# RWKV pairs of a hybrid trunk: two column copies on ScalarE, bonus products emitted later, the inverse's stores on GpSimd's queue

## The chip, the cores and the metric

The kernel runs on one core of one Trainium2 chip. The metric is the device time of one execution in microseconds; lower is better. All data are float32, and the large products are made of three products of float32r halves each.

## What is computed

A trunk of two layers over 1024 tokens of width 1024. Each layer has a token mixer, a cross-attention into 256 memory tokens and a squared-ReLU MLP, each between two RMS norms. The change lies in layer 0's mixer, which runs RWKV-7 beside Mamba-2 behind one input projection. RWKV's part, cut to what matters:

```python
kk = hd(k * k_k);  kk = kk / max(norm(kk), 1e-12)
k  = k * (1.0 + (a - 1.0) * k_a)
def step(S, inp):                      # per head, 64 x 64 state
    r_t, w_t, k_t, v_t, a_t, b_t = inp # a_t = -kk, b_t = kk * a
    sa = einsum('bhvk,bhk->bhv', S, a_t)
    S = S * w_t + sa[..., None] * b_t + v_t[..., None] * k_t
    return S, einsum('bhvk,bhk->bhv', S, r_t)
...
y = y + sum(r_h * k_h * r_k, axis=-1, keepdims=True) * v_h   # the bonus
```

The recurrence is computed in 16 chunks of 64 tokens, with a 64x64 triangular inverse T for each chunk and head. The eight heads are worked on as four pairs of 128 channels.

## The kernel before

`mixer0` first runs 27 projections (`fm`): TensorE (PE) multiplies a weight tile with the normalised input, 48 products of 128x512 for each (`pd<-xth,wb`, `pd<-xtl,wb`; "dense products" below, 1280 in all). While these run, generators do the rest in small pieces. `rw_pair(p)` is the generator of pair p. It makes the decay factors, normalises k (two "norm products" with the block-of-ones matrix `ct`, evicted in L521, then Ln and Exp on ScalarE and a Newton step on VectorE, L490 to L493), forms the chunk operands `va` and `bk` (L534 to L553), multiplies r, k and r_k (L551, L554), and makes the **bonus products** (`rkw` times `xn`, L563), which L564 evicts with the factor v. Then four groups follow, each with eight AB products (`va`, `bk`; L575, evicted in L578) and 32 transposes, all of which `rw_chunk` reads later from DRAM scratch.

In `va[:, :, 1]`, each position of a chunk takes minus kk times the decay up to the position before; the first column of a chunk has no position before it, so it is minus kk alone (L546). `PC` keeps the decay of the whole chunk (L547). Both touch 16 columns, one for each chunk.

`rw_inverse(q)` waits for pairs 2q and 2q+1, loads the triangles (`As`), runs 31 steps of forward substitution on VectorE (L616, L617) and stores T: `Ts` and its transpose `As` (L620), twelve stores in all (L627). `rw_chunk(c)` then loads T of its chunk (L655, L656), and its first product is `cT` with `cAB`. After the projections come layer 1's K and V products of the cross-attention (`memside`; `ph<-mh,wb`), among which the chunks and the Mamba windows (`mb_window`) are interleaved, and then the output projection (`outproj`).

Two things set the order. A generator's `yield` gives a delay on a virtual clock `self.pt`, multiplied by `self.lag` (1.8 here), or a condition; `tick` runs the pieces that are due between two dense products. Then the tile framework's scheduler orders the instructions once more, by priorities that follow the order of emission. Each engine executes its own list strictly in order. DMAs are issued in order as well, by the engine that owns the queue: `nc.sync` (SP), `nc.scalar` (ScalarE, ACT) or `nc.gpsimd` (POOL). A waiting instruction holds whatever stands behind it on its engine.

Of the kernel before, what the change touches and what calls it, by code (L numbers as in the profile page):

```python
# [13 lines left out]
AF = mybir.ActivationFunctionType  # L14
# [7 lines left out]
CH = 64  # L22
# [33 lines left out]
class Trunk:  # L56
# [438 lines left out]
    def rw_pair(self, p, km, rm, va, lora, wa, rm64, pool, pt, S):  # L495


        nc, pc = self.nc, self.pc
        mul, add = ALU.mult, ALU.add
# [13 lines left out]
        v3 = lambda x: x.rearrange("p (c t) -> p c t", t=CH)  # L513
# [18 lines left out]
        va = va[0]  # L532
        eP = va[:, :, 3]
# [4 lines left out]
        kn = nt("xo")  # L538
# [4 lines left out]
        nc.scalar.copy(bk[CH:, :, 2], bk[CH:, :, 0])  # L543
        yield 3.5
        nc.vector.scalar_tensor_tensor(va[:, :, 1, 1:], v3(kn[:])[:, :, 1:], -1.0, eP[:, :, 0:CH - 1], mul, mul)
        nc.gpsimd.tensor_scalar(va[:, :, 1, 0], v3(kn[:])[:, :, 0], -1.0, None, mul)  # L546
        nc.gpsimd.tensor_copy(self.PC[:, p, :], eP[:, :, CH - 1])  # L547
        nc.gpsimd.tensor_tensor(eP, v3(rm[:]), eP, mul)
        k2 = nt("xn")
        nc.scalar.activation(k2[:], a[:], AF.Identity, scale=col(Q_KA), bias=self.oka[:, p:p + 1])  # L550
# [5 lines left out]
        self.st1(S["AR0"][:, :, p].rearrange("c p t -> p c t"), va[:, :, 1])  # L556
        self.st1(S["AR1"][:, :, p].rearrange("c p t -> p c t"), va[:, :, 3])
        yield lambda: 0.0 if self.v_done[0] > p else None
        yield 2.0
        bv = nt("xn")  # L560
        for sl in H:
            ps = self.psm()
# [28 lines left out]
    def rw_inverse(self, q, pool, pt, S):  # L591


        nc = self.nc
        yield lambda: 0.0 if self.rw_done[0] >= 2 * q + 2 else None
        B = 32
        block = lambda s: self.ed.tile([P, B, B], F32, name=self.n(s), tag="xo") if q else pool.tile([P, B, B], F32, name=self.n(s), tag=s)
        As = block("As")
        for a in range(2):
            for j in range(2):  # L600
                src = S["ABK"][:, CH * j:CH * j + CH, 2 * q + a, j, :]
                r0 = 64 * a + 32 * j
                for b in range(2):
                    v = src[:, B * b:B * b + B, B * b:B * b + B]
                    self.ld1(As[r0 + 16 * b:r0 + 16 * b + 16], v)
        Ts = block("Ts")
        yield 9.0
        nc.gpsimd.memset(Ts[:], 0.0)
        nc.gpsimd.memset(Ts[:].rearrange("p i k -> p (i k)")[:, 0:B * B:B + 1], 1.0)
        for k in range(B - 1):  # L610

            if k % 8 == 0:
                pr = pt.tile([P, B, B], F32, name=self.n("pr"), tag="tmp")
            n, m = B - 1 - k, k + 1
            pv = pr[:].rearrange("p i k -> p (i k)")[:, 0:n * m].rearrange("p (i j) -> p i j", j=m)
            nc.vector.tensor_tensor(pv, As[:, k, m:].unsqueeze(2).broadcast_to([P, n, m]), Ts[:, k, :m].unsqueeze(1).broadcast_to([P, n, m]), ALU.mult)  # L616
            nc.vector.tensor_tensor(Ts[:, m:, :m], Ts[:, m:, :m], pv, ALU.add)  # L617
            if k % 2:
                yield 0.4 + 0.004 * n * m
        nc.vector.tensor_copy(As[:], Ts[:].rearrange("p i k -> p k i"))  # L620
        for n_, x in enumerate((Ts, As)):
            for a in range(2):
                for j in range(2):
                    r0 = 64 * a + 32 * j
                    for b in range(n_ + 1):
                        dst = S["T"][n_, :, CH * j + B * b:CH * j + B * b + B, 2 * q + a, B * b:B * b + B]
                        (nc.scalar if b else nc.sync).dma_start(dst, x[r0 + 16 * b:r0 + 16 * b + 16])  # L627
        self.inv_done[0] += 1
        self.inv_t = self.pt + 5.0

# [1222 lines left out]
```

## Time and profile before

| | us |
|---|---|
| median of 3 runs (3078.88 to 3088.8) | 3080.72 |
| the profiled execution, in all | 3086.54 |
| its span, first to last instruction | 3084.8 |
| PE busy | 2924.9 (95%) |
| VectorE (DVE) busy | 1758.5 (57%) |
| ScalarE (ACT) busy | 1318.0 (43%) |
| GpSimd (POOL) busy | 656.5 (21%) |

The table of busy time tells which engine fills the span. A table by stretches tells where PE is not full, and which of its two clock levels was granted: 1.00 stands for 2.4 GHz, 0.50 for 1.2 GHz. The lists of waits and the timelines then name, for each gap of PE, what ended it.

### The profile page before, as it was taken

What the parts mean: (1) busy time and instruction counts of PE and PEld (TensorE: products, weight loads), DVE (VectorE), ACT (ScalarE), POOL (GpSimd) and SP (SyncE); (2) the same over time, 40 slices, a digit from 0 to 9 for tenths busy, and PEclk for the clock granted to TensorE, in tenths of its full rate; (3) what the DMA queues carried; (4) which work ended last, traced back from release to release, by engine and by line L of the source; (5) the groups of instructions that cost most, each with busy time, mean ns of one, the idle gap of its engine ahead of it and who ended that gap; (6) DMA issues with size and microseconds to landing.
All of it is one profiled execution on the core that took longest, in us unless ns stands there. A gap on an engine that the chain in (4) does not pass through costs nothing. (4 is left out here: it accounts for less than half of the span.)

```text
span 3084.8 us, 40050 instructions
## 1 busy us (share of the span) xinstructions
PE 2924.9 (95%) x15652; PEld 2381.1 (77%) x15652; DVE 1758.5 (57%) x2283; ACT 1318.0 (43%) x2096; POOL 656.5 (21%) x648
## 2 busy tenths in 40 slices
PE   8999999889989989999999999899999899999998
PEld 7776677777767867887887778777788678888876
DVE  7255776666643476664757723145653666657476
ACT  6455543445333345444443423133353444454433
POOL 1111131122212124443001200011221334440002
PEclk9999999999999989999999999999999899999999
DMA  7834476678552124447745533446331234468456
GB/s 257 276 88 127 123 197 196 209 255 266 184 186 69 69 89 147 152 151 267 239 138 163 195 106 103 123 132 219 116 129 62 82 120 151 150 217 283 138 164 224
DMA packets 274237, 506.00 MB, mean 164 GB/s; under 512 B 57328, under 2 KB 159664, under 8 KB 274048
## 3 DMA queue, kind: packets, MB, share of 16 engines
q1 hardware_dynamic: 218048, 309.89, 31.8%
q0 software_dynamic: 28448, 108.08, 9.2%
q10 hardware_dynamic: 27552, 85.47, 8.5%
q8 instruction: 123, 2.02, 0.3%
q14 instruction: 66, 0.54, 0.1%
HBM read 348.45 MB, written 154.89 MB: 163 GB/s over the span
## 5 line engine op out<-in xcount | busy, mean ns | idle before, releaser
L201 PE MATMUL pd<-xth,wb 128*128 128x512 f32 x1120 | 362.9, 399 | 1.9 <-DVE wb L218 1.9
L218 DVE TENSOR_TENSOR wb<-wr,wb 128x1024 fp32r<-128x1024 f32 (+1 forms) x148 | 184.0, 1247 | 301.6 <-ACT wb L217 301.0
L201 PE MATMUL pd<-w,sh 128*128 128x512 f32 x1024 | 322.5, 396 | 0.0
L201 PEld LDWEIGHTS pd<-xth,wb 128*128 128x128 f32 x1120 | 210.3, 189 | 56.3 <-issue 7.5
L217 ACT ACTIVATE wb<-wr 128x1024 fp32r<-128x1024 f32 (+1 forms) x148 | 154.6, 1050 | 228.3 <-PE pm L201 170.6
L201 PE MATMUL pd<-T,wb 128*128 128x512 f32 x1008 | 247.9, 391 | 3.2 <-DVE wb L218 3.2
L201 PE MATMUL pd<-xtl,wb 128*128 128x512 f32 (+1 forms) x576 | 227.7, 396 | 0.0
L201 PEld LDWEIGHTS pd<-T,wb 128*128 128x128 f32 x1008 | 188.9, 188 | 45.9 <-DVE wb L218 4.1
L201 PEld LDWEIGHTS pd<-w,sh 128*128 128x128 f32 x1024 | 190.6, 188 | 41.9 <-ACT p L1397 0.3
L201 PE MATMUL pd<-w,sl 128*128 128x512 f32 x512 | 201.9, 394 | 0.0
L201 PE MATMUL pm<-wb,xth 128*128 128x512 f32 x512 | 165.0, 403 | 2.5 <-DVE xtl L218 2.5
L201 PE MATMUL pm<-xb,wb 128*128 128x512 f32 x672 | 166.4, 396 | 0.0
L201 PE MATMUL pm<-wb,wb 128*128 128x512 f32 x672 | 157.1, 389 | 0.2 <-DVE wb L218 0.2
L201 PE MATMUL pm<-T,wb 128*128 128x512 f32 x528 | 137.1, 404 | 13.5 <-ACT T L217 7.6
L201 PEld LDWEIGHTS pm<-xb,wb 128*128 128x128 f32 x672 | 126.4, 188 | 30.1
L201 PEld LDWEIGHTS pm<-wb,wb 128*128 128x128 f32 x672 | 126.0, 188 | 26.7 <-DVE wb L218 0.6
L201 PEld LDWEIGHTS pm<-T,wb 128*128 128x128 f32 x528 | 103.0, 196 | 37.8 <-ACT T L217 8.1
L201 PEld LDWEIGHTS pd<-xtl,wb 128*128 128x128 f32 (+1 forms) x576 | 107.0, 186 | 24.7 <-issue 1.9
L1584 POOL TENSOR_TENSOR ub<-ub 128x512 f32<-128x512 f32 x32 | 49.2, 1538 | 336.9 <-ACT ub L1577 336.9
L201 PE MATMUL pd<-wb,wb 128*128 128x512 f32 x480 | 114.0, 394 | 4.5 <-DVE wb L218 4.4
L218 DVE TENSOR_TENSOR wb<-ws,wb 128x1024 fp32r<-128x1024 f32 x64 | 88.2, 1379 | 52.1 <-ACT wb L217 52.1
L201 PEld LDWEIGHTS pm<-wb,xth 128*128 128x128 f32 x512 | 97.2, 192 | 24.4 <-DVE xtl L218 3.0
(446 smaller groups left out, 6342.6 us busy)
## 6 DMA issues: line engine op xcount, KB each, us to landing
scr<-ub POOLq DMA_DIRECT2D x32, 1792.0 KB, 7.6
ru<-scr SPq DMA_DIRECT2D x112, 512.0 KB, 4.3
rw<-in_ff_dn_dram SPq DMA_DIRECT2D x84, 512.0 KB, 4.6
scr<-xo POOLq DMA_DIRECT2D x39, 512.0 KB, 3.2
scr<-mo POOLq DMA_DIRECT2D x32, 512.0 KB, 5.6
xo<-scr SPq DMA_DIRECT2D x32, 512.0 KB, 3.6
wr<-in_ff_upT_dram SPq DMA_DIRECT2D x32, 512.0 KB, 3.6
wf<-in_ff_upT_dram SPq DMA_DIRECT2D x32, 512.0 KB, 3.6
```

What stands on the lines that cost most here:

```text
L201: self.nc.tensor.matmul(out, lhsT=lhsT, rhs=rhs, start=start, stop=stop, skip_group_check=on)
L217: self.nc.scalar.activation(hi, src, AF.Copy)
L218: self.nc.vector.tensor_tensor(lo, src, hi.bitcast(F32), ALU.subtract)
L1584: op(sl(3), sl(7), sl(2), add)
```

## The change

It makes three edits. The first columns (L546) and the copies into `PC` (L547) go from GpSimd to ScalarE, four of each. The pause ahead of the bonus products is 5.0 in place of 2.0 on the virtual clock (times 1.8). Of the inverse's twelve stores for each q, the four that ScalarE's queue issued are issued by GpSimd's; the eight of SP's queue stay.

```diff
         nc.vector.scalar_tensor_tensor(va[:, :, 1, 1:], v3(kn[:])[:, :, 1:], -1.0, eP[:, :, 0:CH - 1], mul, mul)
-        nc.gpsimd.tensor_scalar(va[:, :, 1, 0], v3(kn[:])[:, :, 0], -1.0, None, mul)
-        nc.gpsimd.tensor_copy(self.PC[:, p, :], eP[:, :, CH - 1])
+        nc.scalar.activation(va[:, :, 1, 0], v3(kn[:])[:, :, 0], AF.Copy, scale=-1.0)
+        nc.scalar.copy(self.PC[:, p, :], eP[:, :, CH - 1])
         nc.gpsimd.tensor_tensor(eP, v3(rm[:]), eP, mul)
...
         yield lambda: 0.0 if self.v_done[0] > p else None
-        yield 2.0
+        yield 5.0
         bv = nt("xn")
...
-                        (nc.scalar if b else nc.sync).dma_start(dst, x[r0 + 16 * b:r0 + 16 * b + 16])
+                        (nc.gpsimd if b else nc.sync).dma_start(dst, x[r0 + 16 * b:r0 + 16 * b + 16])
```

The built programs differ on every engine between the first pair's bonus products and the output projection. Three places follow.

The first place is VectorE's list in pair 1, from the key's normalisation (L539) to the eviction of the bonus products (L564). Before:

```order
L539 SCALAR_TENSOR_TENSOR xo_2230<-km_1852,pc,xn_2106 128x1024
L541 TENSOR_TENSOR xn_2232<-xo_2230,gain_2038 128x1024
L545 SCALAR_TENSOR_TENSOR va_2174<-xo_2230,va_2174 128x16x63
L542 TENSOR_TENSOR bk_2173<-xn_2232,gain_2176 128x16x64
L485 TENSOR_TENSOR va_2174<-va_2174,sh_2263 128x16x64
L218 TENSOR_TENSOR wb_2271<-wr_2269,wb_2271 128x1024
L551 TENSOR_TENSOR xn_2282<-xn_2282,km_1852 128x1024
L553 TENSOR_TENSOR bk_2173<-xn_2282,gain_2176 128x16x64
L485 TENSOR_TENSOR km_2335<-km_2335,sh_2336 128x1024
L218 TENSOR_TENSOR wb_2343<-wr_2341,wb_2343 128x1024
L564 TENSOR_TENSOR xn_2350<-pm_2351,va_2174 128x512
```

The same place after:

```order
L218 TENSOR_TENSOR wb_2271<-wr_2269,wb_2271 128x1024
L539 SCALAR_TENSOR_TENSOR xo_2242<-km_1852,pc,xn_2054 128x1024
L578 TENSOR_TENSOR AB_2152<-pm_2142,ct 128x512
L578 TENSOR_TENSOR AB_2152<-pm_2143,ct 128x512
L541 TENSOR_TENSOR xn_2244<-xo_2242,gain_1980 128x1024
L551 TENSOR_TENSOR xn_2295<-xn_2295,km_1852 128x1024
L542 TENSOR_TENSOR bk_2185<-xn_2244,gain_2188 128x16x64
L553 TENSOR_TENSOR bk_2185<-xn_2295,gain_2188 128x16x64
L545 SCALAR_TENSOR_TENSOR va_2186<-xo_2242,va_2186 128x16x63
L485 TENSOR_TENSOR va_2186<-va_2186,sh_2263 128x16x64
L564 TENSOR_TENSOR xn_2386<-pm_2387,va_2186 128x512
```

The products of k (L551, L553) now stand ahead of L545 and L485, and the weight split `wb_2271` ahead of L539. On PE, the number of dense products between a pair's second norm product and its bonus products was 112, 112 and 114 in pairs 1 to 3; it is 69, 69 and 101 now.

The second place is GpSimd's list in pair 3, around the products r·decay (L548) and r·k (L554). Before:

```order
L546 TENSOR_SCALAR va_3206<-xo_3285 128x16
L547 COPY PC<-va_3206 128x16
L548 TENSOR_TENSOR va_3206<-km_3027,va_3206 128x16x64
L608 MEMSET Ts_3697 128x1024
L609 MEMSET Ts_3697 128x32
L554 TENSOR_TENSOR xn_3337<-xn_3337,km_3027 128x1024
```

The same place after:

```order
L554 TENSOR_TENSOR xn_3379<-xn_3379,km_2928 128x1024
L627 DMA scr_1339<-As_2698 16x32x32 x4
L548 TENSOR_TENSOR va_3287<-km_2928,va_3287 128x16x64
L608 MEMSET Ts_3795 128x1024
L609 MEMSET Ts_3795 128x32
```

L554 now stands ahead of L548, with the first inverse's four stores between them; L546 and L547 are gone.

The third place is PE's list at the end of the projections. `cT` with `cAB` is chunk 0's first product, `pd_4135` (before) and `pd_4095` (after) the last projection. Before:

```order
L201 MATMUL pd_4056<-xtl_109,wb_3976 64x512 x2
L201 MATMUL pd_4056<-xth_108,wb_3976 128x512
L201 MATMUL pm_4180<-cT_4157,cAB_3718 32x32
L201 MATMUL pd_4135<-xth_108,wb_4053 128x512
L201 MATMUL pd_4135<-xtl_109,wb_4053 128x512
L201 MATMUL pm_4180<-cT_4157,cAB_3718 32x32 x4
L201 MATMUL pd_4135<-xth_108,wb_4053 128x512 x2
```

After:

```order
L201 MATMUL pd_4095<-xtl_109,wb_4032 128x512
L201 MATMUL pd_4095<-xth_108,wb_4032 128x512
L201 MATMUL pm_4347<-cT_4284,cAB_3816 32x32 x8
L201 MATMUL pm_4348<-cUV_3820,cAB_3816 64x64 x8
L201 MATMUL ph_4223<-mh_3806,wb_4169 128x256
L201 MATMUL ph_4223<-ml_3807,wb_4169 128x256
```

Chunk 0's first product moved from the start of the last projection to its end. Pair 3's last group of AB products moved too: it stood behind 1000 of the 1280 dense products and stands behind 1065 now. Chunk 15, which stood ahead of the output projection, now stands among its first products.

## Rows read from the trace of the kernel before

**Rows 1.** The page's table of busy time: share of the span, instructions.
```profile
PE 2924.9 (95%) x15652; PEld 2381.1 (77%) x15652; DVE 1758.5 (57%) x2283; ACT 1318.0 (43%) x2096; POOL 656.5 (21%) x648
```
**Rows 2.** By stretches: length, busy PE, PEld, DVE, ACT, POOL; PE clock, DMA share, GB/s.
```profile
350.00:360.00 10.00, 6.67 (x32) 4.73 (x33) 9.62 (x22) 1.94 (x4) 0.00 (x0) 0.83 0.55 166
410.00:420.00 10.00, 6.44 (x21) 3.90 (x19) 9.83 (x10) 1.52 (x2) 7.06 (x5) 0.79 0.92 195
420.00:430.00 10.00, 10.00 (x61) 6.75 (x61) 4.29 (x6) 3.73 (x6) 2.40 (x1) 0.87 0.86 240
525.00:790.00 265.00, 236.20 (x2976) 204.42 (x2975) 161.36 (x314) 119.68 (x264) 51.84 (x61) 0.96 0.74 241
```
**Rows 3.** PE's waits from 300 to 430 us: total, times, longest.
```profile
PE pm L201 <- POOL xn L554: 3.6, 1, 3.6
PE pm L205 <- DVE xn L564: 3.5, 1, 3.5
PE pd L201 <- DVE wb L218: 1.0, 1, 1.0
```
**Rows 4.** Timeline of PE: start, length, operation, count, [idle before it <- releaser].
```profile
443.88 1.12 PE L201 MATMUL pm<-va,bk 64*128 64x128 f32 x16
...
502.89 0.24 PE L201 MATMUL pm<-cT,cAB 32*32 32x32 f32 x2 [3.15 <-DMA cT<-scr]
...
517.32 0.44 PE L201 MATMUL pm<-cT,cAB 32*32 32x32 f32 x16
...
520.86 0.38 PE L201 MATMUL ph<-mh,wb 128*128 128x256 f32 x1 [2.49 <-ACT zs L825]
```
**Rows 5.** The chain that ended last: 48 dense products in a row (start, length).
```profile
2274.38 11.20 PE pd L201 x48
```
**Rows 6.** Timeline of VectorE and GpSimd, the key's chain in pair 1.
```profile
253.00 0.68 DVE L521 TENSOR_SCALAR xn<-pm 128x512 f32<-128x512 f32 x1
...
277.95 1.23 DVE L553 TENSOR_TENSOR bk<-xn,gain 128x1024 f32<-128x1024 f32 x1
...
279.25 2.41 POOL L554 TENSOR_TENSOR xn<-xn,km 128x1024 f32<-128x1024 f32 x1 [3.45 <-DVE bk L553]
```
**Rows 7.** Timeline of ScalarE in pair 1: a table load and its activation.
```profile
254.79 1.28 ACT L524 ACT_TABLE_LOAD   x1
256.08 1.06 ACT L524 ACTIVATE xn<-xn 128x1024 f32<-128x1024 f32 x1
```
**Rows 8.** Timeline of GpSimd and VectorE: pair 3, and one stretched operation in pair 1.
```profile
401.87 7.74 POOL L546 TENSOR_SCALAR va<-xo 128x16 f32<-128x16 f32 x1 [4.79 <-DVE xo L539]
...
409.38 1.23 DVE L553 TENSOR_TENSOR bk<-xn,gain 128x1024 f32<-128x1024 f32 x1
...
414.19 3.01 POOL L554 TENSOR_TENSOR xn<-xn,km 128x1024 f32<-128x1024 f32 x1
...
272.23 3.41 DVE L485 TENSOR_TENSOR va<-va,sh 128x1024 f32<-128x1024 f32 x1
```
**Rows 9.** Line L587, ScalarE's copies: ns min/median/max, first and last start.
```profile
L587 ACT COPY tm<-pm x64: 354/372/393, 221.3 to 451.0; 128x256 f32<-128x256 f32 x64
```
**Rows 10.** ScalarE's queue at the inverse's end; GpSimd's stores of line L473, issue and landing.
```profile
494.93 3.28 ACTq L627 DMA_DIRECT2D scr<-As  x4
498.33 1.01 ACT L823 COPY ze<-pd 128x1024 f32<-128x1024 f32 x1 [14.30 <-DMA scr<-Ts]
...
L473 POOL DMA_DIRECT2D scr<-mo x16: 752/768/872, 83.4 to 714.4; - x16
...
DMA to landing us min/median/max: 4.2/6.2/10.3
```
**Rows 11.** Timeline of VectorE: first and last instruction of the second inverse.
```profile
453.25 0.19 DVE L616 TENSOR_TENSOR pr<-As,Ts 128x31 f32<-128x31 f32 x1 [0.89 <-DMA As<-scr]
...
493.77 1.12 DVE L620 COPY As<-Ts 128x1024 f32<-128x1024 f32 x1
```
**Rows 12.** PE's waits from 525 to 800 us: the longest.
```profile
PE ph L201 <- ACT w L244: 7.6, 1, 7.6
```

## The prediction

> **What bounds the kernel now.** The first view is the page's table of busy time [rows 1]: TensorE (PE) is busy 95% of a span of 3084.8 us, the next engine 57%. So an edit pays only where PE stands idle or runs at its lower clock. The second view is PE's busy time by stretches [rows 2]. The edited code lies between 200 and 790 us: the projections with the four RWKV pairs run up to about 517 us, the sixteen chunks, the Mamba windows and layer 1's K and V products from there to 790. The third view is what PE waited for [rows 3]. Among the pairs it waited twice at a bonus product: 3.5 us near 353 us, where the products behind it waited for the bonus rows' eviction (L564), and 3.6 us near 417 us, where it waited for GpSimd's product r·k (L554). A PE timeline adds the end of the projections: 3.15 us for the inverse T of chunk 0 (L655), and 2.49 us for ScalarE's last SiLU gate (L825) [rows 4]. After the bonus waits the granted clock shows its lower level, 1.2 GHz, for a while: 0.83 over 350 to 360 us, which is 3.4 us at half pace and so about 1.7 us lost; 0.79 and 0.87 over 410 to 430 us, some 6.8 us and 3.4 us lost [rows 2]. That is the whole prize: 7.0 + 5.1 us at the bonus products, 5.6 us and, taken alike, two losses of 1.7 us at the boundary.
>
> The unit in which I count distances on PE is a dense product of 128x512: 48 of them in a row take 11.20 us, and without the last one's tail one step is 0.227 us [rows 5].
>
> **Part 1: bonus products.** The edit makes the generator wait longer before it emits them, but the built order is what counts. By that order the bonus products of pairs 1 to 3 stand 112, 112 and 114 dense products behind the second norm product of their pair before, and 69, 69 and 101 after. They come nearer to what they depend on, not farther. In exchange the chain that feeds them is shorter: VectorE's k products (L551, L553) move ahead of L545, L485 and, in pairs 1 and 2, of one weight split.
>
> Take pair 1. In the trace the chain runs from L521's second piece at 253.0 us over L553 at 278.0 to the end of GpSimd's L554 at 281.7: 28.7 us [rows 6]. Between L521 and L490 stood three ScalarE activations of 1.06 us, each with a table load of 1.28 us [rows 7]; now two stand there. In the new order the chain from L490 to L553 is twelve VectorE steps of about 1.2 us (one of them 0.7), two evictions of AB and one weight split included: 13.8 us. With 0.7 us for L521, 4.7 for the two activations, 0.3 between them and 2.4 for L554 that is 21.9 us. PE reaches the bonus product after 69 × 0.227 = 15.7 us of dense work and, between it, two groups of pair 0 (16 AB products at 1.12 us [rows 4], their transposes and the switches between forms, about 2.2 us): some 18 to 19 us. So PE would wait about 2.9 us where it waited for nothing. Pair 2 goes alike: 3.5 us in place of 3.45. In pair 3, 24 VectorE steps with inverse's small rows between them and one stall by GpSimd make 31.8 us against 27.5 us on PE: 4.3 us in place of 3.56. The sum of waits is 10.7 against 7.0. Each of the two waits was followed by 3.4 us or more at half clock; at 1.7 us lost for each of three I leave the loss at 5.1 us. **Term: +3.7 us.** Bounds: -12.1 us if PE never waits; +16 us if pair 1's chain keeps its 28.7 us (28.7 - 19 = 9.7 us of wait), pair 2's does the same, and pair 3 waits 3.6 again (23 - 7).
>
> PE also waited 1.0 us for a weight split (L218) among these rows [rows 3]; in pairs 1 and 2 that split now stands three to five steps earlier. **Term: -1 us**, between 0 and -1.
>
> **Part 2: the first columns.** Eight instructions on 16 columns leave GpSimd for ScalarE. One of them took 7.74 us on GpSimd, 401.9 to 409.6 us, and held L548 and with it pair 3's L554, which began at 414.2 although its input was ready at 410.5 [rows 8]. On ScalarE, idle 57% of the span, eight copies of 16 columns cost at most 0.35 us each (the shortest copies here, 128x256, take 0.37 [rows 9]) and stand behind L484, where nothing of PE's waits. The gain of about 4 us for pair 3 is in the chain above, since L554 now stands ahead of L548. The term by itself is 0.
>
> In this trace a VectorE operation of 1.2 us takes 3.41 us where it meets one of GpSimd's [rows 8]. The Trainium skill, "SBUF — State Buffer", section "Who interferes with whom", puts this down to one port pair that is locked for a whole instruction, and its section "SBUF: two separate sides" warns of DMAs issued from GpSimd, whose descriptors are written through that pair. By that rule part 2 helps and part 3 may hurt; the latter is a rival below.
>
> **Part 3: inverse's stores.** Eight stores leave ScalarE's queue, where each set of four stood behind the inverse's end: ScalarE's next piece came 14.3 us late, after four issues of 3.28 us together [rows 10]. They go to GpSimd's in-order queue: the first set stands between L554 and L548 of pair 3, the second ahead of the last SiLU product. GpSimd's strided stores of K take 0.77 us to issue and 6.2 us to land [rows 10]; four of them 3.1 us. Behind the first set waits L548, and behind it pair 3's AB products, which now stand 90 dense products (20 us) behind the bonus product: covered. Behind the second set waits the last L826, which needs ScalarE's L825 anyway. What waits for the second set's landing is chunk 0's second product, which in PE's order now stands behind 100-odd K products of 256 columns, at half a step each some 12 us: due near 529 us, where the stores land near 513. Covered too. So moving the issue costs 0, and frees ScalarE.
>
> **The boundary.** Pair 3's last AB product stands 65 dense products later than before (1065 against 1000): 14.7 us, plus whatever part 1 shifts. The inverse of pairs 2 and 3 took 40.5 us, 453.25 to 493.77 [rows 11], with five convolution steps of 1.28 us among it; in the new order these five are gone: about 34 us. So T is final near 493.8 + 14.7 - 6.4 = 502.1 us; the trace has 9.1 us from there to the first product that uses it, which gives 511.2. PE gets there after all dense products now: 517.3 less 3.15 of wait, 1.7 of clock and 1.3 of chunk products that moved behind, 511.2. Part 1 shifts both alike. The two meet, give or take 3 us. Then ScalarE needs 3.5 us for the last gate before the next products, as before. One wait of about 3 us stays where two stood. **Term: -4 us**, between -7 and +1.
>
> **Chunks.** From 525 to 790 us PE was idle for 265 - 236.2 = 28.8 us [rows 2], in many waits, and once 7.6 us for layer 0's output weights at 792 [rows 12]. The whole interleaving is dealt anew; it holds the same work. Before, the last chunk ended ahead of the output products; now chunk 15 stands among the first of them and can fill part of the 7.6 us. **Term: -2 us**, with 8 us to either side for waits that move, a little more than that longest one. Behind 960 us the order is nearly the same: 0.
>
> **Sum.** +3.7 - 1 - 4 - 2 = -3.3 us. The profiled execution took 3086.5 us in all, 1.7 us more than its span and 5.8 us more than the median of 3080.7. 3086.5 - 3.3 = 3083.2; less 5.8 that is 3077.4, told as 3077.
>
> **Rivals.** *Faster:* PE never waits at a bonus product (-12.1), the split comes in time (-1), the boundary gives 5 and the 7.6 us wait is half filled (-4): -22 us, 3059; half of that gives 3070. For it speaks that the 7.74 us stall is gone, against it that PE comes 43 dense products nearer. Chance of over 0.3% (9.2 us): 0.30.
>
> *Slower, at the bonus products:* the VectorE chain stays as long as it was, since table loads and stalls by GpSimd fill what the new order saves. Then +16 - 1 - 2 = +13 and 3094, or 3090 where the boundary's 4 us come all the same. It decides from about 8 us of wait in each of pairs 1 and 2. Against it: L551 and L553 do stand earlier. Chance 0.10.
>
> *Slower, at the stores:* GpSimd's issue is held as L546 was, 7.74 us, four times: 31 us from 503, and 6 each for the landing and for the load of T, so 546, where chunk 0's second product is due near 529: 17 us and a low clock, less 3.3: +15, 3096. It decides from about 6 us for each issue, where 9 us are lost; none of GpSimd's sixteen issues in that row took over 0.87. Chance 0.06. The Trainium skill's rule named above ("SBUF — State Buffer") is what would make it so.
>
> *The order changes and the time doesn't:* the forecast itself, which also covers that part 3's relief of ScalarE reaches nobody. Chance 0.54.
>
> **Chances.** A measurement of this kernel can tell about 0.3%. Faster by more 0.30, within 0.54, slower 0.16. The range takes in the faster case down to 19 us below the median of before and the slower ones to their near end, where a tenth is left out on either side: 3062 to 3090.
>
> **What would show it.** The waits of PE on L554 or L564: about 3, 3.5 and 4 us in pairs 1 to 3. No GpSimd row of L546 or L547, and L554 right behind L553. L627 on GpSimd near 0.8 us each. Chunk 0's first product behind the last dense one, with a wait of under 4 us. PE's idle time from 525 to 790 us within 8 us of 28.8. I am wrong where that last number moves by more, since I can't derive it, or where PE waits over 7 us at one bonus product.

## The result, and the profile after

The changed kernel takes 3053.73 us (median of 3046.02 to 3058.78), the kernel before 3080.78 in the same series: a ratio of 0.9898, 95% interval 0.9882 to 0.9914. It is faster by 27 us. The forecast was 3077, "within 0.3%", and the measured time lies below its range of 3062 to 3090; the rival *Faster* came true, with 5 us more than its own sum gave.

The table of busy time after, to be read against [rows 1] (same columns):

```profile
PE 2916.2 (96%) x15652; PEld 2377.6 (78%) x15652; DVE 1748.5 (57%) x2283; ACT 1314.5 (43%) x2101; POOL 654.5 (21%) x648
```

PE does the same 15652 instructions in 8.7 us less of busy time, at a mean granted clock of 0.981 in place of 0.977, and 25 us less of idle time. Where, the span cut at three events shows: the start of the second piece of pair 1's norm (L521), the first K product (`ph<-mh`), and the first exponential of layer 0's cross-attention (L1397). The columns are the stretch, its length, PE busy (instructions), granted clock, DMA share and GB/s. First before, then after:

```profile
0.00:253.00 253.00, 235.37 (x1344) 0.99 0.60 198
253.00:520.90 267.90, 253.40 (x1351) 0.97 0.57 159
520.90:934.80 413.90, 363.77 (x3560) 0.94 0.66 218
934.80:3084.80 2150.00, 2072.39 (x9400) 0.98 0.45 150
```
```profile
0.00:251.20 251.20, 234.76 (x1325) 1.00 0.60 197
251.20:501.70 250.50, 244.64 (x1337) 1.00 0.61 169
501.70:913.10 411.40, 369.81 (x3592) 0.93 0.66 219
913.10:3051.00 2137.90, 2066.95 (x9400) 0.99 0.45 152
```

The profiled executions differ by 33.8 us, 6.8 more than the medians do: the one before lay 5.8 us above its median, the one after 1.0 below. Of the 33.8, 1.8 are ahead of anything that was edited, **17.4 in the pairs**, 2.5 in the middle, and **12.1 behind 935 us**, where no line of the kernel was changed. I had expected 1.3 less in the pairs (+3.7 - 1 - 4), 2 in the middle and nothing behind. Some 1.1 us of the 17.4 is work that moved into the middle: 32 of the chunks' small products.

PE's waits from 240 to 430 us after (in all, times, longest), to be read against [rows 3], are the whole list:

```profile
PE pm L205 <- ACT gain L510: 1.4, 1, 1.4
PE pm L201 <- POOL xn L554: 0.6, 1, 0.6
```

The waits of 3.6 and 3.5 us are gone (the 1.4 us at pair 2's transposes, for ScalarE's L510, are new), and so is the lower clock behind them; these are the stretches of [rows 2] after:

```profile
350.00:360.00 10.00, 10.00 (x54) 7.28 (x53) 9.45 (x21) 6.14 (x7) 0.00 (x0) 1.00 0.01 2
410.00:420.00 10.00, 10.00 (x46) 8.29 (x45) 5.26 (x5) 4.13 (x4) 2.40 (x1) 1.00 0.85 243
420.00:430.00 10.00, 10.00 (x73) 7.75 (x73) 3.68 (x5) 5.42 (x8) 2.37 (x1) 1.00 0.49 149
525.00:790.00 265.00, 238.78 (x2935) 204.83 (x2934) 167.43 (x324) 123.62 (x273) 52.40 (x62) 0.93 0.73 239
```

At the boundary [rows 4] two waits stay, of 1.27 and 1.15 us where 3.15 and 2.49 stood (PE's timeline: start, length, what, the idle time before it):

```profile
499.50 0.44 PE L201 MATMUL pm<-cT,cAB 32*32 32x32 f32 x16 [1.27 <-DMA cT<-scr]
...
501.70 0.38 PE L201 MATMUL ph<-mh,wb 128*128 128x256 f32 x1 [1.15 <-ACT zs L825]
```

### The profile page after: what moved, and what is told of

It reads as the page before. It is cut to its first block, busy times and chain, and to the rows that moved or that the text cites. A ratio compares the mean times of both kernels' runs of the same rounds, so it can differ in the third digit from the quotient of the medians.

```text
span 3051.0 us, 40033 instructions
## 1 busy us (share of the span) xinstructions
PE 2916.2 (96%) x15652; PEld 2377.6 (78%) x15652; DVE 1748.5 (57%) x2283; ACT 1314.5 (43%) x2101; POOL 654.5 (21%) x648
## 5 line engine op out<-in xcount | busy, mean ns | idle before, releaser
L201 PEld LDWEIGHTS pd<-w,sl 128*128 128x128 f32 x512 | 96.6, 189 | 21.5
```

The costliest lines, as they stand in the source:

```text
L201: self.nc.tensor.matmul(out, lhsT=lhsT, rhs=rhs, start=start, stop=stop, skip_group_check=on)
```

## The experiments

The kernel before was timed anew in each of three series, at 3082.0 (first four runs), 3087.2 (next four) and 3092.0 us (last three), so ratios are compared. The table has each kernel's ratio, and the lengths of the stretches above in its profiled execution. A length is that of one execution: the five kernels whose PE list is that of before up to 935 us differ by 3 us in the pairs and by 6 in the middle (before, columns, stores, both, other late list).

| kernel | ratio, 95% | pairs | middle | late |
|---|---|---|---|---|
| before | | 267.9 | 413.9 | 2150.0 |
| changed | 0.9898 (0.9882 to 0.9914) | 250.5 | 411.4 | 2137.9 |
| pause alone | 0.9896 (0.9880 to 0.9912) | 253.3 | 409.8 | 2136.6 |
| columns alone | 1.0011 (1.0000 to 1.0021) | 270.8 | 410.5 | 2144.8 |
| stores alone | 1.0005 (0.9994 to 1.0016) | 269.2 | 413.8 | 2149.9 |
| columns and stores | 1.0012 (0.9997 to 1.0026) | 270.9 | 411.1 | 2150.7 |
| before, later splits | 0.9970 (0.9958 to 0.9982) | 268.8 | 403.8 | 2148.7 |
| changed, pause 4.0 | 0.9920 (0.9896 to 0.9944) | 254.9 | 415.8 | 2140.4 |
| changed, pause 8.0 | 0.9964 (0.9950 to 0.9978) | 263.9 | 426.1 | 2142.6 |
| before, pause 2.5 | 0.9988 (0.9973 to 1.0003) | 259.4 | 428.0 | 2138.5 |
| before, other late list | 0.9989 (0.9976 to 1.0003) | 267.9 | 416.8 | 2145.2 |
| changed, late list of before | 0.9943 (0.9931 to 0.9955) | 250.5 | 417.1 | 2154.9 |
| changed, pause 6.0 | 0.9944 (0.9931 to 0.9957) | 255.6 | 421.2 | 2143.3 |

### Which of the three edits

In the built programs PE's list follows the pause alone: with the pause of 2.0 it is that of before, with 5.0 that of the changed kernel, whatever engine the columns and stores are on. So the edits can be taken one by one. *Theory A*: the new order that the pause makes, PE's above all, carries the gain. *Theory B*: GpSimd's and ScalarE's relief carries it.

The pause alone:
```diff
-        yield 2.0
+        yield 5.0
```


> Only the pause ahead of the bonus products is longer (5.0 for 2.0); columns and stores stay on the engines of before. PE's list is then that of the changed kernel, word for word. Theory A (PE's new order carries the gain): 3050 to 3062 us, that is 19 to 31 less than before; PE waits under 1.5 us at each bonus product, no stretch of lower clock stands between 340 and 430 us, and the 13.1 us wait near 904 us is not there. Theory B (the relief of GpSimd and ScalarE carries it): 3073 to 3082; L546 still takes several us on GpSimd in a pair, and PE waits 3 us or more at a bonus product or at chunk 0. Theory C (each edit gives a part of its own): 3062 to 3073.

The columns alone (L546 and L547 on ScalarE):
```diff
-        nc.gpsimd.tensor_scalar(va[:, :, 1, 0], v3(kn[:])[:, :, 0], -1.0, None, mul)
-        nc.gpsimd.tensor_copy(self.PC[:, p, :], eP[:, :, CH - 1])
+        nc.scalar.activation(va[:, :, 1, 0], v3(kn[:])[:, :, 0], AF.Copy, scale=-1.0)
+        nc.scalar.copy(self.PC[:, p, :], eP[:, :, CH - 1])
```


> Only the first columns and the copies into PC go to ScalarE; PE's list is that of before, word for word. Theory A: 3073 to 3082; the 3.56 us wait at pair 3's bonus product goes (the 7.74 us stall of L546 stood ahead of it) and with it one stretch of lower clock, some 3.6 + 3.4 = 7 us at most; the wait near 353 us, the boundary and the 13.1 us near 904 us stay. Theory B: 3060 to 3070. Theory C: 3068 to 3075.

The stores alone:
```diff
-                        (nc.scalar if b else nc.sync).dma_start(dst, x[r0 + 16 * b:r0 + 16 * b + 16])
+                        (nc.gpsimd if b else nc.sync).dma_start(dst, x[r0 + 16 * b:r0 + 16 * b + 16])
```


> Only the inverse's four stores for each q move from ScalarE's queue to GpSimd's; PE's list is that of before. Theory A: 3077 to 3084, no change: ScalarE's 14.3 us behind the first inverse held nobody PE waits for. Theory B: 3065 to 3075. My rival of the prediction, the slow issue on GpSimd: 3090 or more, L627 at 6 us or more each.

Columns and stores together, the pause of before (the two diffs above):

> Both engine moves, without the longer pause: PE's list is that of before. Theory A: 3072 to 3082, the same as the columns alone. Theory B: 3050 to 3062, all of the gain. Theory C: 3064 to 3074.

Theory A holds. The pause alone gives 0.9896, all three edits 0.9898; the two moves give nothing, alone or together. (The three kernels without the pause came 2 to 5 us above the ranges that A gave them: I had allowed the columns up to 7 us, and they gave none.) With the pause alone, L546 and L547 are back on GpSimd, and PE's two waits from 240 to 430 us are the same 1.4 and 0.6 us. My sign that no lower clock stands from 340 to 430 us failed there: 0.83 over 360 to 370 us, behind the 1.4 us. The pause reorders the lists of all engines, and no run changes PE's alone; that PE's order matters most is read from its waits.

The columns alone are instructive, because they do take away the 7.74 us of L546 [rows 8], and PE waits as long as before. Its waits from 300 to 440 us, then pair 3 on GpSimd's and VectorE's timeline:

```profile
PE pm L205 <- DVE xn L564: 5.2, 2, 3.4
PE pm L201 <- POOL xn L554: 1.6, 1, 1.6
```
```profile
409.70 6.02 POOL L548 TENSOR_TENSOR va<-km,va 128x1024 f32<-128x1024 f32 x1
...
413.38 3.42 DVE L553 TENSOR_TENSOR bk<-xn,gain 128x1024 f32<-128x1024 f32 x1
```

The stall went to the next instruction in GpSimd's list: L548 takes 6.02 us while VectorE's L553, which L554 waits for, takes 3.42 instead of 1.2. Of the 3.56 us wait 1.6 stays, and 1.75 comes at L564. The rows fit the rule that the prediction weighed: by the Trainium skill ("SBUF — State Buffer", section "Who interferes with whom"), a VectorE product with both inputs in SBUF contends with a GpSimd instruction that reads SBUF, and one of the two is blocked for a whole instruction. L548's end, 415.72 us, less the 2.4 us that it takes elsewhere is 413.3, where L553 begins; L553 is then 2.2 us longer than usual. What frees the chain in pair 3 is that L554 stands ahead of the slow neighbour, and the pause alone does that: L554 begins at 397.66 us there, ahead of L546 (400.01 us, 0.29 long) and L548. The rival at the stores did not come: GpSimd issues four in 2.60 us after (0.65 each, 399.89 us), against my price of 3.1.

### The wait at the start of the cross-attention

Near 904 us PE stood idle for 13.09 us before, a row that I had not read. VectorE's timeline there, with PE's next product:

```profile
892.25 2.36 DVE L218 TENSOR_TENSOR w<-wr,w 128x1024 fp32r<-128x1024 f32 x2 [9.72 <-ACT w L217]
894.53 6.89 DVE L218 TENSOR_TENSOR w<-kr,w 128x1024 fp32r<-128x1024 f32 x6
902.15 1.28 DVE L334 SCALAR_TENSOR_TENSOR xn<-x,r,gain 128x1024 f32<-128x1024 f32 x1 [0.72 <-POOL r L307]
904.55 1.28 DVE L334 SCALAR_TENSOR_TENSOR xn<-x,r,gain 128x1024 f32<-128x1024 f32 x1 [1.12 <-POOL r L307]
905.75 1.28 DVE L341 TENSOR_TENSOR y<-ph,gain 128x512 f32<-128x512 f32 x2
...
903.58 0.88 PE L205 MATMUL pm<-ct,xn 128*128 128x128 f32 x3 [13.09 <-DVE xn L334]
```

The last output product's evictions (L341), which free PSUM for the scores, stand behind eight splits of key tiles and two norms; PE's wait of 13.09 us ends with the first of these norms. In the changed kernel they stand behind two splits:

```profile
883.47 2.36 DVE L218 TENSOR_TENSOR w<-wr,w 128x1024 fp32r<-128x1024 f32 x2 [3.29 <-ACT w L217]
885.75 1.28 DVE L341 TENSOR_TENSOR y<-ph,gain 128x512 f32<-128x512 f32 x2
...
887.18 1.19 PE L201 MATMUL pd<-w,sh 128*128 128x512 f32 x2 [4.59 <-DVE y L341]
```

To see what this place is worth by itself, the kernel before with only the later key tiles held back:
```diff
+        if l == 0:
+            for k in range(2, NK):
+                nc.vector.tensor_scalar(kp[k][0][:, 0:1], self.last_y[:, D - 1:D], 0.0, None, ALU.mult)
         for k in range(NK):
             self.weights(KP[k], into=kp[k], raw=...)
```


> The kernel before, with one thing changed far behind the edit: six one-column copies make the splits of the last six key tiles of the first cross-attention wait for the last output product's eviction (L341), so that in VectorE's list this eviction stands behind two splits and two norms, not behind eight splits and two norms; ScalarE's copies of these tiles move behind its two squares in the same way. PE's list stays that of before. Theory A2 (some 5 of the 28 us come from that one place, dealt anew by the scheduler, and have nothing to do with the pairs): the wait of 13.1 us near 904 us falls to 5 to 8 us, and the time by 4 to 8 us, to 3073 to 3078. Rival: the wait is set by the loads of the key tiles and only moves: 3079 to 3086.

The wait is 6.28 us, the middle 10 us shorter, the ratio 0.9970 (9 us); expected were 4 to 8. So this wait came from the order of VectorE and ScalarE, not from the loads:

```profile
896.84 1.94 PE L205 MATMUL pm<-ct,xn 128*128 128x128 f32 x8 [6.28 <-DVE xn L334]
```

### Other pauses: is it the place of the bonus products, or luck?

Pause 4.0 in the changed kernel (`yield 4.0` for `yield 5.0`):

> The changed kernel with a pause of 4.0 in place of 5.0. The bonus products of pairs 1 to 3 stand where the changed kernel has them (528, 720 and 912 dense products in), the list elsewhere differs. Theory A (the pairs' part is a matter of where these stand): no wait over 1.5 us at a bonus product, no stretch of lower clock from 340 to 430 us, chunk 0's first product near 500 us; in all 3048 to 3066, since the rest is dealt anew. Rival (5.0 met by luck): a wait of 3 us or more at a bonus product, or 3070 and more.

Pause 8.0:

> The changed kernel with a pause of 8.0. The bonus products stand 86, 165 and 73 dense products behind the second norm product in pairs 1 to 3 (69, 69 and 101 with 5.0), and the last AB product of pair 3 stands 48 dense products (11 us) later. Theory A: pair 3's chain is met by PE, with 2 to 8 us of wait there, and the inverse ends some 10 us later, so that chunk 0 waits 5 to 12 us where the changed kernel waits 1.3: 3062 to 3085. Rival (later is better): 3045 to 3056.

Pause 2.5 in the kernel before, columns and stores untouched (`yield 2.5` for `yield 2.0`):

> The kernel before with a pause of 2.5 in place of 2.0, nothing else. The distances of the bonus products are 102, 119 and 113 in pairs 1 to 3 (112, 112 and 114 before), in another order around them; the last AB product stands 97 dense products (22 us) later than before. Theory A: waits of 2 to 4 us stay at two bonus products, and chunk 0 waits 3 to 10 us: 3075 to 3092. Rival (any new order of this list takes 20 us away, since before was an unlucky one): 3055 to 3068.

Pause 6.0 in the changed kernel:

> The changed kernel with a pause of 6.0 in place of 5.0. The bonus products of pairs 1 and 2 stand where the changed kernel has them, those of pair 3 99 dense products (22 us) later, and so the last AB product 30 later (7 us). Theory A: no wait at a bonus product; T is late by some 6 us, and chunk 0 waits 3 to 8 us where the changed kernel waits 1.3; the rest dealt anew: 3052 to 3070. Rival (later is better): below 3050.

With 4.0 the pairs keep most of their gain (254.9 us; waits of 1.65 and 1.45 at the bonus products of pairs 2 and 3, clock 1.00), a little over the 1.5 I had allowed in one of them. With 6.0 the pairs gain as well, 17 us are left in all, and the late T is there, at the upper end of the 3 to 8 us I gave it:

```profile
506.56 0.64 PE L201 MATMUL pm<-cT,cAB 32*32 32x32 f32 x16 [8.17 <-DMA cT<-scr]
```

With 8.0 the median fell in the range, but not for my reason: pair 3's L554 ended at 420.0 us and PE came at 421.0, so nothing waited there, and chunk 0's first product stands only at 548.3 us; what waited, 3.5 us for ScalarE's last gate, was PE's first K product. The profiled execution, 9 us above this kernel's median, loses 13 us against the changed kernel in the pairs, where PE waits elsewhere (2.2 us for AB, L578, 1.9 for a split, 1.8 for L484) and the clock is 0.97, and 15 us in the middle. With 2.5 the waits at the bonus products stay (6.7 us in two, L564), and the pairs' and the late stretch's gains of 8.5 and 11.5 us are eaten by a middle of 428.0; some 2 of the 8.5 are 64 chunk products that moved there. So "any other order is 20 us better" is wrong: with pauses of 4.0 to 6.0 the pairs take 250 to 256 us, with 2.0, 2.5 and 8.0 259 to 271, and the middle is dealt between 410 and 428 us with no rule that I could read ahead of the run.

### The stretch behind 935 us

The code emits the same work in the same order there. Yet PE's list differs in some twenty places between before and after, the first near 1770 us, and the kernels with pauses of 2.5, 4.0 and 8.0 have the changed kernel's list there (4.0 with one further difference). In the table their late stretches are 2136.6 to 2142.6 us, those with the list of before 2144.8 to 2150.7. The kernel with 6.0 has a mixture: the order of before near 1770 us, that of the changed kernel from 2127 us on, and 2143.3 us. To test it, a few products of PE that nobody reads, behind the scores, tip the scheduler from one late list to the other and leave the list ahead as it is (four of them in the kernel before, eight in the changed one):
```diff
+        if l == 0:
+            for _ in range(2):
+                d = self.psm()
+                for _ in range(2):
+                    nc.tensor.matmul(d[:], lhsT=kp[0][0][:, 0:128], rhs=kp[0][0][:, 0:512], start=True, stop=True)
         kc.close()
```


> The kernel before plus four products of 128x512 on PE behind the scores of the first cross-attention, whose result nobody reads (some 0.9 us of work). Up to there its list is that of before; from there on the scheduler gives the late list of the changed kernel, nothing else is changed. Theory A3 (the list behind 935 us comes in two versions, and the changed kernel's is some 9 us shorter): from the first scores' exponentials (L1397) to the end 9 us less than before, in three places: ahead of layer 1's V products near 1787 us, in the mLSTM windows near 2139 us, and behind 2450 us; in all 3071 to 3076, that is 6 to 10 us less than before. Rival (the later part follows the earlier one, through what is still under way): 3079 to 3086.

> The changed kernel plus eight such products at the same place (1.8 us of work). Up to there its list is that of the changed kernel, from there on the scheduler gives the late list of the kernel before. Theory A3: 7 to 13 us more than the changed kernel, 3060 to 3068. Rival: 1 to 3 us more, 3053 to 3058.

The changed kernel with the late list of before loses 0.45% (0.9943 against 0.9898), some 14 us, and 17.0 us in the profiled stretch, 1.8 of them the added products: theory A3, and more than expected. The other way round only 4.8 us come in the stretch (5.7 without the added 0.9), and the ratio of 0.9989 can't be told from 1; I had expected 6 to 10.

Two waits follow the list both ways: PE on `xtl` ahead of layer 1's V products, 2.5 us before, and on G of the mLSTM windows (L1214). From some 1730 to 2470 us they read, in the changed kernel with the old late list:

```profile
PE pm L201 <- DVE G L1214: 3.9, 2, 3.0
...
PE pm L201 <- DVE xtl L218: 2.9, 1, 2.9
```

and in the kernel before with the other one, where no wait on `xtl` is listed:

```profile
PE pm L201 <- DVE G L1214: 1.8, 2, 0.9
```

The mixture of 6.0 fits: 1.4 us on `xtl` and 1.8 on G. Cut between the same instructions of PE's list, around the V products and around the windows, the two places read as follows (columns as above, behind PE those of PEld, DVE, ACT and POOL): before, after, and the kernel before with the other late list.

```profile
1765.30:1885.10 119.80, 117.26 (x514) 94.34 (x513) 34.65 (x35) 36.52 (x51) 8.66 (x19) 0.98 0.35 118
2110.20:2150.10 39.90, 33.71 (x175) 25.43 (x174) 22.10 (x65) 12.15 (x42) 9.50 (x14) 0.96 0.48 166
```
```profile
1744.10:1858.90 114.80, 114.80 (x513) 92.82 (x512) 34.01 (x35) 36.54 (x51) 9.11 (x20) 1.00 0.37 123
2084.10:2119.70 35.60, 32.65 (x175) 24.76 (x174) 24.00 (x65) 12.27 (x42) 9.59 (x14) 1.00 0.52 182
```
```profile
1770.80:1886.20 115.40, 115.40 (x514) 93.25 (x513) 34.27 (x35) 36.57 (x51) 9.14 (x20) 0.99 0.37 123
2112.10:2147.80 35.70, 32.74 (x175) 24.80 (x174) 24.04 (x65) 12.27 (x42) 9.64 (x14) 1.00 0.62 182
```

In all thirteen kernels the first place takes 115 to 116 us with the changed kernel's order and 118 to 121 with that of before, the second 36 to 37 and 38 to 41; the kernel with 6.0 is on the old side at the first and on the new side at the second. So the late list is shown to matter at these places, in the kernel before as in the changed one. By the means it is worth 6.6 us there, and 9.5 in the whole stretch (without the mixture, added products taken off). Less those products the two ratios allow 0 to 8 us and some 6 to 18; that the list gives one kernel less than the other is not shown.

## Why the prediction was wrong

**Part 1: the step that failed.** I had PE reach pair 1's bonus product 18 to 19 us behind the norm, and the chain 21.9 us long, so that PE would wait 2.9 us. The timelines of PE, VectorE and GpSimd after:

```profile
250.15 1.02 PE L201 MATMUL pm<-xn,ct 128*128 128x512 f32 x2
...
272.25 1.45 PE L201 MATMUL pm<-xn,rkw 128*128 128x512 f32 x3
...
251.21 0.69 DVE L521 TENSOR_SCALAR xn<-pm 128x512 f32<-128x512 f32 x1 [1.24 <-PE pm L201]
255.84 1.23 DVE L490 TENSOR_TENSOR u<-xn,xn 128x1024 f32<-128x1024 f32 x1 [3.94 <-ACT xn L525]
...
268.23 1.22 DVE L553 TENSOR_TENSOR bk<-xn,gain 128x1024 f32<-128x1024 f32 x1
...
269.53 2.41 POOL L554 TENSOR_TENSOR xn<-xn,km 128x1024 f32<-128x1024 f32 x1 [12.59 <-DVE bk L553]
```

PE takes 22.1 us, and L554 ends at 271.94, 0.3 us ahead of it. The VectorE part was right (13.6 us from L490 to the end of L553; I had 13.8). The start is 4.6 us where I had 5.7, because ScalarE's first table load ran beside L521 (251.08 to 252.36 us). PE's part was too short by 3 us. Its groups between the two events (records, busy time, mean ns):

```profile
L201 PE MATMUL pd<-xth,wb 128*128 128x512 f32 x46 | 15.4, 401 | 0.0
L201 PE MATMUL pd<-xtl,wb 128*128 128x512 f32 x23 | 9.2, 399 | 0.0
L201 PE MATMUL pm<-va,bk 64*128 64x128 f32 x32 | 2.6, 283 | 0.0
L205 PE MATMUL pm<-ct,va 64*128 64x64 f32 x16 | 1.4, 235 | 0.0
L205 PE MATMUL pm<-ct,bk 64*128 64x64 f32 x16 | 1.3, 232 | 0.0
L201 PE MATMUL pm<-xn,ct 128*128 128x512 f32 x2 | 1.0, 592 | 0.0
```

The 69 dense products are as counted (46 and 23; their records overlap, so the step of 0.227 stands: 15.7 us). Beside them lie 6.3 us: 2.6 of AB products, where I had 1.1 (one group's 16 records stood for two groups), 2.7 of transposes for 2.2, and the norm's own 1.0, which I had left out on PE's side and on the chain's. So 2 us too little on PE and 1 too much in the chain, in numbers near 20, turned a wait of 2.9 us into none. Pair 2 meets within 0.6 us in the same way. In pair 3 PE needs 33.1 us, 367.16 to 400.27 (I had 27.5), and the chain 28.6 (31.8). Measured, the waits at the bonus products and their evictions fell from 7.0 to 0.6 us, 1.4 came new for L510, and the clock's loss fell from 5.1 to 0: -10.1, next to the bound of -12.1 that I had set as a rival and not the +3.7 I took.

**The split** gave 1.9 us among the pairs, but 1.5 us came back at another one near 487 us. **The boundary** was right: 3.2 us of wait and 1.7 of clock, 4.9 against 4. **Parts 2 and 3** were right at 0, in either order.

**Chunks.** Idle time from 525 to 790 us is 26.2 us (28.8 before), within the 8 us given. But the term left out the clock: the granted clock there fell from 0.96 to 0.93, and over the whole middle PE's busy time rose by 6.0 us, some 1 of it the 32 products that moved in. The idle time fell by 8.5 us; the place near 904 us gave more than that (18.0 us of wait there before, 13.1 and 4.9; 8.3 after, 2.8, 4.6 and 0.9). The middle's -2.5 is next to the predicted -2 by two things that I had not seen, so by luck, and it is smaller than the 6 us by which executions of one list differ there.

**Behind 960 us** I wrote "the order is nearly the same: 0". It was not the same: 12.1 us in this pair of executions, some 9.5 by the means of all kernels. This and Part 1 are the whole miss: with -10.1 and -12.1 in place of +3.7 and 0 my sum gives -29.2 (-26.6 with 9.5), against the 27 measured.

## What to carry to other kernels

Where a chain and the engine that needs it come within a few microseconds, count every instruction of that engine between the two events in the rows, small groups and the first event's own too, and give the meeting an even chance on both sides: 3 us in each pair stood between my +4 and the measured -10. Where a scheduler makes the order, compare the built lists to the last instruction, not to the last edited line: an unedited place may carry a third of the result, and a wait like 13 us behind eight weight splits is found by reading the longest waits of the whole span first. Moving one slow instruction off a contended engine may only hand its stall to the next one in the list.

## What the runs showed of the hardware

PE's granted clock fell to 1.2 GHz behind the waits of 3.45 and 3.56 us before [rows 2, 3]. Behind single waits of 1.4 to 1.7 us among the dense products it went either way. It stayed at its upper level behind 1.65 and 1.45 us with the pause of 4.0 (1.00 over 330 to 350 and 400 to 420 us). Behind the same wait for L510, with the same PE list, it stayed there in the changed kernel (1.36 us) and fell with the pause alone (1.39 us), in this order, with the columns of [rows 2]:

```profile
360.00:370.00 10.00, 8.63 (x52) 5.62 (x51) 6.79 (x16) 5.52 (x8) 0.00 (x0) 1.00 0.50 157
```
```profile
360.00:370.00 10.00, 8.61 (x34) 5.32 (x34) 7.44 (x17) 4.63 (x7) 0.00 (x0) 0.83 0.52 157
```

With the columns alone, two waits of 1.6 and 1.75 us 7 us apart were followed by the lower level as well, 0.88 over 420 to 430 and 0.77 over 430 to 440 us. Over the pairs the difference holds all the same: the six executions with PE's list of before show 10 to 14 us at the lower level, those with pauses of 4.0, 5.0 and 6.0 none, and the pause alone 3.4.

GpSimd's 128x1024 product L789, 2.38 us at the median of its eight, took 7.13 us at 384.80 us after, among a dense run of VectorE's work. So stalls of this size were not removed by the change; none stood in the way of L554.

The same eight stores of T (64 KB each) are cut otherwise by the two queues. The queue table before and after (packets, MB, share; q10 is ScalarE's queue, q0 GpSimd's):

```profile
q0 software_dynamic: 28448, 108.08, 9.2%
q10 hardware_dynamic: 27552, 85.47, 8.5%
```
```profile
q0 software_dynamic: 28704, 108.61, 9.5%
q10 hardware_dynamic: 23328, 84.95, 8.4%
```

ScalarE's queue made 4224 packets of them, 528 for each store, and GpSimd's 256, 32 for each. The time did not change by it.
